# Sending part of one store over half of the DMA engines in a batched matrix product

## The chip, the cores and the metric

The kernel runs on one core of a Trainium2 chip. The metric is the device time of one execution in microseconds (us). The kernel before takes 136.39 us (median of three runs, 136.19 to 136.42). A profile times the core's own span, which is 1.7 to 1.95 us shorter than the device time of the same execution: 134.6 us for the kernel before. Whenever two spans are compared here, they are spans of single profiled executions; when two times are compared, they are medians of several executions.

## The reference

```python
def setup_inputs():
    batch, dim_i, dim_j, dim_k = 32, 256, 512, 384
    return {
        "x": np.random.randn(batch, dim_i, dim_j).astype(np.float32),
        "y": np.random.randn(batch, dim_j, dim_k).astype(np.float32),
    }

def reference(x, y):
    return np.einsum('bij,bjk->bik', x, y).astype(np.float32)
```

Thirty-two independent products, 16.8 MB of `x` and 25.2 MB of `y` read, 12.6 MB written.

## The kernel before

The 32 products are done in 16 units of two (`u` is the unit, `G = 2`). Loads and stores are all issued by SyncE in one fixed order, so they form one queue. `x` is loaded for four products at once (2 MB), `y` for one product (0.79 MB), and each unit is stored by one DMA of 128 partitions (0.79 MB). In between the inputs are rounded to 16 bits, `x` is transposed on TensorE, and the products are collected from PSUM. None of that is touched by the change.

```python
    def load(u):
        if u == 0:
            load_x(0)
        if (u + 1) * G % Q == 0 and u + 1 < U:
            load_x((u + 1) * G // Q)
        y_of[u] = y_pool.tile([P, G, NJ, K], F32, name="y_sb")
        for g in range(G):
            keep(nc.sync.dma_start(out=y_of[u][:, g],
                                   in_=y[u * G + g].rearrange("(q t) k -> q t k", q=P)))
    ...   # round_x, transpose, round_y, multiply, collect
    def store(u):
        keep(
            nc.sync.dma_start(
                out=out[u * G : (u + 1) * G].rearrange("g (m e) k -> (g m) e k", e=NE),
                in_=o_of.pop(u),
            )
        )

    ahead = LAG - 2
    for u in range(ahead):
        load(u)
    for s in range(U + 2):
        if s + ahead < U:
            load(s + ahead)
        ...   # the work of unit s - 1, and the collection of unit s - 2
        if s >= 2:
            store(s - 2)
```

Each DMA has one of eight completion semaphores, in turn: DMA n uses slot n modulo 8, and SyncE does not issue it before DMA n-8 has landed. This comes from the framework and is seen in the program; no line of the kernel says it.

## Time and profile before

| what | before |
|---|---|
| device time | 136.39 us |
| span of the profiled execution | 134.6 us |
| DMA packets, bytes | 8072, 54.64 MB |
| rate over the span | 406 GB/s |
| busiest compute engine | PE, 61% |
| last store: issued, first engine landed, last engine landed | 128.73, 131.81, 133.30 us |
| from that last landing to the end of the span | 1.33 us |

The first row is the median of the timed runs, the next four are on the page, the last from the trace's records of issues and landings. The prediction below shows the page's DMA row, the chain and the last windows. Two more lines of before turn out to matter, from the view of one source line, which here is the end of the program. The columns are the engine, the instruction and its count, then shortest/median/longest duration in ns, and the first and last start in us.

```profile
L223 SPq EVENT_SEMAPHORE  x7: 17/28/28, 129.1 to 134.6; - x7
...
L223 SPq DRAIN  x3: 7/7/130, 133.7 to 134.2; - x3
```

SyncE closes the program with waits on the completion semaphores and some drains. The first drain starts at 133.7, though the last store landed at 133.3.

### The profile page before, as it was taken

The page shows a single profiled execution, that of the slowest core. Times are in us where ns is not written, and L with a number is a line of the kernel's source. Part 1 is how long each engine was busy: PE and PEld are TensorE (multiplying, and loading weights), DVE is VectorE, ACT ScalarE, POOL GpSimd, SP SyncE. Part 2 cuts the span into 40 slices and gives each one's busy share as a digit, 9 for nine tenths or more (in the row PEclk, how much of TensorE's full clock was granted, in tenths as well). Part 3 has the DMA queues.
Part 4 walks back from the last instruction along what each step waited for, and adds up shares of the span by engine and source line. Part 5 has one row for each costly group of instructions (what it writes and reads, how often), then busy time and mean ns, then how long its engine had stood idle before and what let it go on. Part 6 is the DMA issues. An engine that isn't in the chain of part 4 may idle for free.

```text
span 134.6 us, 1741 instructions
## 1 busy us (share of the span) xinstructions
PE 82.4 (61%) x640; PEld 58.9 (44%) x640; DVE 57.6 (43%) x144; ACT 75.6 (56%) x145; POOL 0.7 (1%) x6
## 2 busy tenths in 40 slices
PE   0029496965197929785197853964469652896900
PEld 0018374854064717563164632652246531565500
DVE  0034457363633563515624256352453536427510
ACT  3046687576662876538744378552774557629600
POOL 2000000000000000000000000000000000000000
PEclk9999999999658996899757997799757998569985
DMA  5999999999999999999999999999999999999991
GB/s 112 419 403 454 403 424 421 456 392 412 420 451 410 414 427 422 455 392 418 425 444 438 400 412 427 458 403 414 425 420 443 413 414 427 420 427 422 417 405 74
DMA packets 8072, 54.64 MB, mean 406 GB/s; under 512 B 896, under 2 KB 896, under 8 KB 7040
## 3 DMA queue, kind: packets, MB, share of 16 engines
q1 hardware_dynamic: 8064, 54.53, 97.5%
q8 instruction: 5, 0.08, 0.2%
q14 instruction: 3, 0.02, 0.1%
HBM read 41.94 MB, written 12.58 MB: 405 GB/s over the span
## 4 chain that ended last, share of the span: by engine, by line
DMA 91%; PE 2%; DVE 1%; SPq 1%; issue 0%
DMA y_sb<-in_y_dram 62%; DMA x_sb<-in_x_dram 15%; DMA out_dram<-o_sb 13%; PE o_ps L145 2%; DVE o_sb L162 1%; SPq L85 0%; DVE y_r L133 0%; SPq L70 0%; SPq L167 0%
## 5 line engine op out<-in xcount | busy, mean ns | idle before, releaser
L145 PE MATMUL o_ps<-y_r,xt_sb 128*64 128x384 f16 x512 | 60.0, 400 | 29.8 <-DVE o_sb L162 27.8
L145 PEld LDWEIGHTS <-xt_sb 128*64 128x64 f16 x512 | 40.5, 133 | 45.6 <-issue 32.2
L131 ACT CAST y_r<-y_sb 128x384 f16<-128x384 f32 x64 | 29.5, 512 | 16.8 <-DMA y_sb<-in_y_dram 16.7
L133 DVE CAST y_r<-y_sb 128x384 f16<-128x384 f32 x64 | 20.0, 356 | 30.2 <-DMA y_sb<-in_y_dram 28.8
L113 PE MATMUL t_ps<-identity,x_r 128*128 128x128 f32 x128 | 23.1, 319 | 15.9 <-DVE x_r L95 15.9
L113 PEld LDWEIGHTS t_ps<-identity,x_r 128*128 128x128 f32 x128 | 18.4, 210 | 23.2 <-issue 12.8
L97 ACT CAST x_r<-x_sb 128x1024 f16<-128x1024 f32 x16 | 15.9, 1043 | 19.3 <-DMA x_sb<-in_x_dram 19.3
L123 ACT COPY xt_sb<-t_ps 128x512 f16<-128x512 f16 x32 | 17.4, 588 | 14.3 <-DVE xt_sb L121 13.9
L95 DVE CAST x_r<-x_sb 128x1024 f16<-128x1024 f32 x16 | 10.4, 690 | 25.3 <-DMA x_sb<-in_x_dram 25.3
L121 DVE COPY xt_sb<-t_ps 128x512 f16<-128x512 f16 x32 | 13.0, 422 | 13.8 <-PE t_ps L113 13.2
L162 DVE COPY o_sb<-o_ps 128x384 f32<-128x384 f32 x32 | 16.4, 549 | 1.8 <-PE o_ps L145 1.8
L160 ACT COPY o_sb<-o_ps 128x384 f32<-128x384 f32 x32 | 14.1, 500 | 1.2 <-PE o_ps L145 1.2
L97 ACT ACT_TABLE_LOAD x1 | 1.3, 1283 | 0.7 <-PEq L212 0.7
masks.py:199 POOL TENSOR_SCALAR_AFFINE_SELECT identity<-identity 128x128 f32<-128x128 f32 x1 | 0.3, 292 | 0.1
masks.py:197 POOL MEMSET identity<- 128x128 f32 x1 | 0.2, 204 | 0.3 <-POOLq L212 0.3
L212 POOL MEMSET const-bfloat16-1.0<- 128x1 bf16 x1 | 0.1, 101 | 0.0
L212 POOL MEMSET const-uint8-127<- 128x1 uint8 x1 | 0.1, 101 | 0.0
L212 POOL MEMSET const-float32-0.0<- 128x1 f32 x1 | 0.1, 98 | 0.2 <-issue 0.2
L212 POOL MEMSET const-float32-1.0<- 128x1 f32 x1 | 0.1, 98 | 0.0
## 6 DMA issues: line engine op xcount, KB each, us to landing
y_sb<-in_y_dram SPq DMA_DIRECT2D x32, 768.0 KB, 17.9
x_sb<-in_x_dram SPq DMA_DIRECT2D x8, 2048.0 KB, 20.8
out_dram<-o_sb SPq DMA_DIRECT2D x16, 768.0 KB, 17.8
```

Source lines behind the costliest of these rows:

```text
L95: keep(nc.vector.tensor_copy(xr_of[q][:, r : r + 2], x_of[q][:, r : r + 2]))
L97: keep(nc.scalar.copy(xr_of[q][:, r : r + 2], x_of[q][:, r : r + 2]))
L113: nc.tensor.transpose(t_ps[:, f, h], x_w[:, h * NE + e + f, n::NW], identity)
L121: keep(nc.vector.tensor_copy(dst[:, f], src[:, f]))
L123: keep(nc.scalar.copy(dst[:, f], src[:, f]))
L131: keep(nc.scalar.copy(yr_of[u][:, g, t], y_sb[:, g, t]))
L133: keep(nc.vector.tensor_copy(yr_of[u][:, g, t], y_sb[:, g, t]))
L145: nc.tensor.matmul(o_ps[g * M : (g + 1) * M], xt_sb[:, t // 2, e, a * PQ : (a + 1) * PQ, :, t % 2].rearrange("c p h -> c (p h)"), y_r[:, g ...
L160: keep(nc.scalar.copy(o_of[u][:, e], ps_of[u][e]))
L162: keep(nc.vector.tensor_copy(o_of[u][:, e], ps_of[u][e]))
L212: nc = _bacc.Bacc("TRN2", target_bir_lowering=False, num_devices=1)
```

## The change

The intent is to move work from the upper eight DMA engines to the lower eight. In the fifth store, the last 32 partitions go in four DMAs of 8 partitions, and a DMA of 8 partitions is to be carried by engines 0 to 7 alone (the prediction says where this comes from). The remaining 96 partitions use all sixteen.

```diff
+SHARE, SMALL = 4, 4
 ...
     def store(u):
-        keep(
-            nc.sync.dma_start(
-                out=out[u * G : (u + 1) * G].rearrange("g (m e) k -> (g m) e k", e=NE),
-                in_=o_of.pop(u),
-            )
-        )
+        o_sb = o_of.pop(u)
+        dst = out[u * G : (u + 1) * G].rearrange("g (m e) k -> (g m) e k", e=NE)
+        cuts = (0, *range(P - SMALL * 8, P + 1, 8)) if u == SHARE else (0, P)
+        for k, m in enumerate(cuts[:-1]):
+            rows = slice(m, cuts[k + 1])
+            keep(nc.sync.dma_start(out=dst[rows], in_=o_sb[rows]))
```

## The prediction

> **What bounds the kernel now.** I read the page first: the 40 slices, then the chain of work that ended last.
>
> ```profile
> PEclk9999999999658996899757997799757998569985
> DMA  5999999999999999999999999999999999999991
> GB/s 112 419 403 454 403 424 421 456 392 412 420 451 410 414 427 422 455 392 418 425 444 438 400 412 427 458 403 414 425 420 443 413 414 427 420 427 422 417 405 74
> ...
> HBM read 41.94 MB, written 12.58 MB: 405 GB/s over the span
> ## 4 chain that ended last, share of the span: by engine, by line
> DMA 91%; PE 2%; DVE 1%; SPq 1%; issue 0%
> ```
>
> The DMA row is at nine tenths in 38 of 40 slices and the rate is flat at about 423 GB/s (the windows view: 423 for 20 to 60 us, 424 for 60 to 100, 423 for 100 to 124). No compute engine is busy over 61% of the span. The reader is to see that the sixteen DMA engines are the bound from the second slice to the last but one, and that the change moves no byte more or less: 54.5 MB stay 54.5 MB. So it can matter only through which engine carries what.
>
> Then the chain in order of time:
>
> ```profile
> 34.70 17.89 DMA y_sb<-in_y_dram
> 52.58 0.02 issue
> 52.60 17.86 DMA y_sb<-in_y_dram
> 70.47 0.02 issue
> 70.48 0.03 SPq L167
> 70.51 0.03 issue
> 70.54 17.84 DMA out_dram<-o_sb
> 88.38 0.02 issue
> 88.40 20.84 DMA x_sb<-in_x_dram
> 109.24 0.02 issue
> 109.26 14.84 DMA y_sb<-in_y_dram
> 124.10 0.02 issue
> ```
>
> Each DMA is issued 0.02 to 0.07 us after an earlier one has landed. Numbering the 56 DMAs in order of issue, DMA n starts when DMA n-8 has landed on its last engine; the trace shows eight completion semaphores used in turn. About 17.9 us lie between issue and landing, so the queue is eight deep and never dry.
>
> Last, the end of the span by windows (PE, PEld, DVE, ACT, POOL busy, clock, DMA share, GB/s):
>
> ```profile
> 128.00:130.00 2.00, 0.06 (x2) 0.00 (x0) 0.56 (x1) 0.00 (x0) 0.00 (x0) 1.00 0.94 393
> 130.00:131.00 1.00, 0.00 (x0) 0.00 (x0) 0.00 (x0) 0.00 (x0) 0.00 (x0) 0.58 1.02 424
> 131.00:132.00 1.00, 0.00 (x0) 0.00 (x0) 0.00 (x0) 0.00 (x0) 0.00 (x0) 0.50 0.69 283
> 132.00:133.00 1.00, 0.00 (x0) 0.00 (x0) 0.00 (x0) 0.00 (x0) 0.00 (x0) 0.50 0.16 68
> ```
>
> The rate does not stop, it fades over about 1.5 us: the engines do not finish together. The trace keeps sixteen landing records for each DMA, one per engine, without the engine's number. For the last store but one they lie, from the earliest (129.49 us), at 0, .13, .13, .25, .30, .31, .42, .59, .72, .97, 1.37, 1.52, 1.52, 1.75, 1.76 and 1.99 us. In the first DMAs this spread is 0.65 us. It jumps to 2.06 at the eleventh DMA, after a 16,384-byte packet on the instruction queue that started at 31.74 us and took 1.09; four more such packets follow (54.6, 77.9, 103.4, 125.7 us), and more engines fall behind. As no engine is ever idle, one that has fallen behind stays behind. The last store lands first at 131.81 and last at 133.30: the slowest engine sets the end. It also sets the last y load's landing (122.16 first, 124.10 last), on which the last products, the last store's issue (128.73) and so the whole tail hang.
>
> **What the Trainium skill says.** "DMA: Bandwidth & Descriptors", section "Why a DMA increments its semaphore by 16 and not by 1", says that a DMA issued from SyncE runs on the largest number k up to 16 that divides its slowest dimension, and on the lowest-numbered k engines. So 128 and 96 partitions use all sixteen, and 8 partitions use engines 0 to 7. The trace of before agrees for 128 (sixteen landings for each DMA); it has none with 8. Section "Latency and other measured facts" of that page calls engines 7 and 15 usually slower, and holds the cause uncertain. This trace has several slow engines but no numbers for them, so it cannot confirm it; 7 and 15 lie one in each half, which would speak against a gain. "Runtime: NRT & Kernel Launch", section "Instruction fetch mechanics", says that instructions are refilled in blocks of 16 KiB by DMA; the five 16,384-byte packets agree. No page says which engine carries a refill.
>
> **The change part by part.** Removed: one store of 128 partitions, eight packets of 6,144 bytes on each of 16 engines. Such a packet takes 234 ns (median of the trace) and overlaps the next by 4, so one costs its engine 230 ns.
> - Added: a store of 96 partitions, 6 packets on each engine, and four of 8 partitions, one packet on each of engines 0 to 7. The lower half carries 10 packets instead of 8, the upper half 6. That is +2 x 0.230 = +0.46 us for each lower engine and -0.46 us for each upper one.
> - Completion writes: DMA follows DMA on an engine at 1.88 us, less 8 x 0.230 = 1.84 leaves about 0.04 each. The lower half has four more: +0.16 at most. So about +0.5 to +0.62 us below, -0.46 above.
> - Issue: four more DMA instructions on SyncE at 0.34 each, 1.4 us. SyncE stands waiting for slots most of the time here, so this costs nothing.
> - Slots: the five pieces take five of the eight. The x load now issued at 56.34 must wait for the DMA that lands at 66.79, a delay of 10.4 us. At 66.79 the queue still holds two y or store DMAs of 0.79 MB and the fifth store, 2.36 MB; at 424 GB/s that is 5.6 us. So it doesn't run dry. After the fifth store's landing at about 72.3 several slots come free together, the loads catch up, and the order is as before. No gap, no cost.
>
> What is left is the shift between the halves, early enough (the data moves at 68 to 72 us) to be carried to the end by an always full queue. Its worth depends on which half the late engines are in. If the eight latest (0.72 to 1.99) are the upper half, the upper maximum becomes 1.99 - 0.46 = 1.53 and the lower 0.59 + 0.6 = 1.2: the end comes 0.46 us earlier, at about 135.9. The lateness list splits well at that place, and a change that relieves just this half would be odd unless somebody had seen it late. I give this six or seven chances in ten. Perfect balance could not bring more than the mean lateness: 1.99 - 0.86 = 1.1 us.
>
> **The rivals.**
> - The late engines are mixed. Then the slowest of the lower half, say 1.76, becomes about 2.3 and the end comes 0.3 us later: 136.7. For it: five instruction packets would fall on one half only by some rule, none of which I can see. Against it: the intent of the edit.
> - The slowest engine is in the lower half: 1.99 + 0.6, so 137.0. Same evidence, less likely.
> - The loss of queue depth bites: a gap at 66 to 70 us. Then each us of gap is a us at the end. Against it are the 5.6 us worked out above; I give it 4%.
> - A floor beside the engines: the last store is issued at 128.73 and lands 3.08 us later even on an engine that had run dry. But its issue hangs on the last y load's slowest engine as well, so both move together. With an early y landing the gain is not eaten.
>
> **Range and chances.** Weights of 0.65 for 135.9, 0.2 for 136.7 to 137.0, and the rest near 136.4 (a partial gain, with another late engine taking over) give a mean of about 136.1. Three runs of before lie within 0.23 us, so noise adds 0.15. Eight times in ten: 135.7 to 136.9. Two per cent are 2.7 us; the shift is 0.46 and even perfect balance 1.1, so over 2% faster is all but excluded. Over 2% slower needs a dry queue.
>
> **What the changed profile would show.** Sixty DMAs on the page instead of 56; the stores' issues x20. The x load that followed the fifth store is issued at about 66.8 instead of 56.34, and the DMA row and GB/s stay flat there; a digit under 9 around 66 to 72 us would prove the rival of depth. If the upper half is the late one, the last y load lands at about 123.6 instead of 124.10, the last store is issued near 128.3, and the fade at the end is shorter by some 0.4 us. If not, the fade is longer, and the last y lands later. The prediction is wrong beyond its range if small DMAs carry a fixed cost on their engines that the 0.04 us doesn't show, or if the instruction packets fall elsewhere in the changed program.

## The result

The changed kernel takes **137.03 us** (median of six runs, 136.31 to 137.16) beside 136.34 for the kernel before (six runs, 136.19 to 136.43). The ratio is 1.0041, with a 95% interval of 1.0017 to 1.0064. A ratio is computed as the mean time of one kernel's fast runs over that of the other's of the same rounds, so it isn't quite the ratio of the medians. The kernel is slower by about half a us, where I had expected 0.3 us less.

The page of the changed kernel, the lines that answer to those in the prediction:

```profile
DMA  5999999999999999999999999999999999999991
GB/s 121 413 401 454 410 419 420 452 395 420 412 459 394 419 423 431 434 403 421 425 425 440 406 422 419 447 428 408 421 425 443 413 412 426 425 423 426 417 388 64
DMA packets 8104, 54.64 MB, mean 405 GB/s; under 512 B 928, under 2 KB 928, under 8 KB 7072
```

The DMA row is the same digit for digit, and there is no hole at 66 to 72 us (slices 20 to 22: 425, 425, 440). The 32 added packets are the completion writes of four DMAs on eight engines each; so the four small DMAs ran on eight engines, as the page of the Trainium skill on DMA that the prediction cites says. The bytes are unchanged.

The order of issue, from SyncE's timeline of the changed kernel (start, duration, line):

```profile
54.27 10.66 SPq L175 DMA_DIRECT2D out_dram<-o_sb  x5
66.54 0.37 SPq L73 DMA_DIRECT2D x_sb<-in_x_dram  x1
```

The five pieces are issued over 10.7 us, and the x load after them at 66.54 instead of 56.34, as predicted (66.8). It costs nothing, since the queue still holds work.

One warning on reading this profile. A DMA on eight engines leaves nine records on its semaphore, one about 0.45 us after the start of its issue and eight landings, instead of sixteen. The page then gives no landing for any DMA of the four semaphores that carried such a piece, 28 of the 60. Its chain of waits and its "us to landing" for the changed kernel are therefore not used here. The landing times below are the trace's own records, grouped by the number of engines of each DMA. An engine's lateness is the time from the first landing of a DMA to the landing on that engine.

The windows at the end of the changed kernel, to be set against those of before in the prediction:

```profile
130.00:131.00 1.00, 0.00 (x0) 0.00 (x0) 0.00 (x0) 0.00 (x0) 0.00 (x0) 1.00 0.99 412
131.00:132.00 1.00, 0.00 (x0) 0.00 (x0) 0.00 (x0) 0.00 (x0) 0.00 (x0) 1.00 0.82 338
132.00:133.00 1.00, 0.00 (x0) 0.00 (x0) 0.00 (x0) 0.00 (x0) 0.00 (x0) 1.00 0.19 80
```

The fade is a little later (0.82 against 0.69 of the DMA time from 131 to 132), where the prediction wanted it earlier. The last landing is at 133.37 us, 0.07 later than before. But the span is 134.88 against 134.63, 0.25 longer. So 0.18 us were lost in the tail, the time from the last landing to the end of the span. The closing lines of the changed kernel:

```profile
L227 SPq EVENT_SEMAPHORE  x7: 17/28/28, 133.4 to 134.8; - x7
...
L227 SPq DRAIN  x3: 7/7/7, 134.1 to 134.4; - x3
```

All seven semaphore waits of SyncE now start after the last landing (133.4), where before the first of them started at 129.1. The first drain is at 134.1 instead of 133.7. Here are the starts of the closing instructions, from the trace's instruction records, in us:

```
                               before    changed
last store landed              133.30    133.37
wait that the landing ended    133.32    133.39   (slot 8 of 8; slot 4 of 8)
next instruction               133.75    133.84   (a drain;     the wait on slot 5)
waits on slots 6, 7, 8         -         133.92, 133.99, 134.06
drains                         133.75, 133.94   134.13, 134.19
end of span                    134.63    134.88
```

SyncE waits for the eight slots in a fixed order. With 56 DMAs the last store has the last slot, so nothing is left to wait for. With 60 DMAs it has the fourth slot, and four more waits follow, 0.07 us each, although all are already met. (Of these 0.28 us only 0.18 show in the tail, because the first drain takes 7 ns here and 130 ns before.) In both kernels there is also a pause of about 0.43 us just after the landing; this is looked into below.

### The profile page after: what moved, and what is told of

The parts are those of the page before. It is cut to its first block, busy times and chain, and to the rows that moved or that the text cites. A ratio compares the mean times of both kernels' runs of the same rounds, so it can differ in the third digit from the quotient of the medians.

```text
span 134.9 us, 1747 instructions
## 1 busy us (share of the span) xinstructions
PE 80.8 (60%) x640; PEld 58.6 (43%) x640; DVE 57.3 (42%) x144; ACT 75.6 (56%) x145; POOL 0.7 (1%) x6
## 4 chain that ended last, share of the span: by engine, by line
DMA 82%; PE 7%; DVE 3%; SPq 2%; issue 1%
DMA y_sb<-in_y_dram 56%; DMA x_sb<-in_x_dram 15%; DMA out_dram<-o_sb 11%; PE o_ps L148 6%; SPq L88 2%; DVE o_sb L165 1%; DVE xt_sb L124 1%; SPq L73 1%; DVE y_r L136 1%; PE t_ps L116 1%; SPq L175 0%
## 5 line engine op out<-in xcount | busy, mean ns | idle before, releaser
L148 PE MATMUL o_ps<-y_r,xt_sb 128*64 128x384 f16 x512 | 57.5, 388 | 29.4 <-DVE o_sb L165 27.4
L148 PEld LDWEIGHTS <-xt_sb 128*64 128x64 f16 x512 | 39.7, 129 | 43.7 <-issue 31.6
L116 PE MATMUL t_ps<-identity,x_r 128*128 128x128 f32 x128 | 23.9, 324 | 17.9 <-DVE x_r L98 17.8
L116 PEld LDWEIGHTS t_ps<-identity,x_r 128*128 128x128 f32 x128 | 18.9, 209 | 25.4 <-issue 12.8
```

Source lines behind the costliest of these rows:

```text
L116: nc.tensor.transpose(t_ps[:, f, h], x_w[:, h * NE + e + f, n::NW], identity)
L148: nc.tensor.matmul(o_ps[g * M : (g + 1) * M], xt_sb[:, t // 2, e, a * PQ : (a + 1) * PQ, :, t % 2].rearrange("c p h -> c (p h)"), y_r[:, g ...
```

## The experiments

Theories. **A**: moving packets shifts the lateness of the two halves, and late engines are in the lower half too. **B**: the cost is in the number of DMAs (slots, completions, a shallower queue). **C**: the lateness comes from instruction refills that fall on fixed engines. **D**: part of the cost is in the closing instructions.

### Is it the shift or the number of pieces?

The first batch, with eleven runs of the kernel before (median 136.47).

**e1_even**: the same number of pieces, each over all sixteen engines.

```diff
-        cuts = (0, *range(P - SMALL * 8, P + 1, 8)) if u == SHARE else (0, P)
+        cuts = (0, *range(P - SMALL * 16, P + 1, 16)) if u == SHARE else (0, P)
```

> The fifth store in five DMAs again (64 partitions, then four of 16), so as many DMAs and completion slots as in the changed kernel, but each piece runs on all sixteen engines: 4 + 4 x 1 = 8 packets on each, no shift between the halves. Theory A (the cost of the change is the two extra packets on each lower engine, which lengthens the work of an engine that is already late): no different from before, 136.3 to 136.5 us. Theory B (the cost is the four added DMAs: completions, slots, a shallower queue): as slow as the changed kernel, 136.9 to 137.1.

Measured: 137.34 us, ratio 1.0048 (1.0023 to 1.0072). Theory A, as I had put it, missed: pieces without a shift are as slow as the change. The trace gives three parts. The pieces themselves cost almost nothing: from the y load before the store to the x load after it, the mean landing of the engines moves by 6.79 us, against 6.71 before; the latest engine's moves by 6.73 against 6.72. The closing instructions cost 0.21 us. The rest, 0.76 us of the profiled execution, came at 126 us, long after the store, when an instruction refill fell on an engine that was already 1.36 us late and made it 2.82. So this kernel is slow for reasons other than its pieces.

**e2_two**: the change made in the fifth and in the tenth store.

```diff
-        ... if u == SHARE else (0, P)
+        ... if u in (SHARE, SHARE + 5) else (0, P)
```

> The same cut of a quarter into four DMAs of 8 partitions, in the fifth and in the tenth store: twice the shift, four packets more on each lower engine, four fewer on each upper one. Theory A: the late lower engine is 1.1 us later than in the kernel before, the end comes 1.1 to 1.3 us later, about 137.5; the landing records of the last stores are spread over more than 3 us. Theory B: also about 137.7, but without that spread. The late engines being all in the upper half (my prediction): below 136.

Measured: 137.20 us, ratio 1.0051 (1.0019 to 1.0084). The expected 137.5 was roughly met, but not with theory A's sign: the last store but one is spread over 2.15 us, not over more than 3. The second cut is close to the end, and the loads behind it were issued later: the first y load after that store, which the kernel before issues at 98.86 us, is issued at 109.79. Its windows from 112 to 118 us (last columns: clock, DMA share, GB/s):

```profile
112.00:114.00 2.00, 0.59 (x3) 0.28 (x3) 0.92 (x4) 1.17 (x4) 0.00 (x0) 0.55 1.08 399
114.00:116.00 2.00, 0.62 (x5) 0.42 (x7) 1.70 (x5) 1.93 (x5) 0.00 (x0) 0.50 0.96 396
116.00:118.00 2.00, 2.00 (x16) 1.31 (x14) 0.26 (x1) 0.61 (x2) 0.00 (x0) 0.50 1.02 399
```

The kernel before has in the same windows:

```profile
112.00:114.00 2.00, 0.00 (x0) 0.00 (x0) 1.01 (x4) 1.07 (x4) 0.00 (x0) 0.77 1.02 427
114.00:116.00 2.00, 1.11 (x8) 0.81 (x10) 1.21 (x3) 1.82 (x4) 0.00 (x0) 0.50 1.02 427
116.00:118.00 2.00, 2.00 (x16) 1.30 (x14) 0.63 (x2) 0.93 (x2) 0.00 (x0) 0.50 1.01 421
```

27 GB/s are missing over 6 us, 0.16 MB or 0.4 us of the full rate. I first took this for the rival of queue depth, but a dry queue is not what the trace shows: the DMA share of these windows is 1.02 on average in both kernels, and the page of e2 has no digit under 9 there:

```profile
DMA  5999999999999999999999999999999999999992
```

What differs is the length of packets. Between 112 and 122 us, 18 packets of 6,144 bytes took 0.4 to 2.3 us instead of 0.234, in all 8.2 us more, or 0.5 us for each of the sixteen engines; the kernel before has none there. Why they took longer, and whether the late issue has a part in it, is not shown. At this cut too the shift is seen: between the y loads around it the latest landing moved by 4.17 us instead of 3.72, the earliest by 3.22 instead of 3.68. The last store lands at 134.31, 1.0 us later than before; but its span is only 0.5 longer, as its tail is 0.83 us instead of 1.33. That was the first sign of theory D: with 64 DMAs the last store has the last slot again, and the pause is gone.

**e3_half**: two small DMAs instead of four (`SHARE, SMALL = 4, 2`).

> Two DMAs of 8 partitions instead of four, in the fifth store only: half the shift, one packet (0.23 us) more on each lower engine. Theory A with a slowest engine in the lower half: 0.25 to 0.35 us over before, about 136.65. If the slowest is in the upper half and the next, 0.2 to 0.3 us earlier, in the lower: within 0.1 us of before.

Measured: 136.53 us, ratio 1.0012 (0.9988 to 1.0036), no difference from before. The time fits the second branch of what was expected, but the trace does not: at the cut the latest engine, 1.71 us late, was in the lower half and the next, 1.61, in the upper. The latest landing was pushed out by 0.24 us there, half of what four pieces do (see the table below), and still the last store landed at 133.30, as before. So the shift at the cut did not reach the end in this trace.

**e4_map**: the kernel before with tiny loads that name the engines.

```diff
+        for k in ((2 * u - 5, 2 * u - 4) if 3 <= u <= 9 else (15,) if u == 10 else ()):
+            mark = const_pool.tile([k, 128], F32, name=f"mark{k}")
+            keep(nc.sync.dma_start(out=mark, in_=x[0][:k, :128]))
```

> The kernel before with fifteen tiny loads of 1, 2, ... 15 partitions of 512 bytes between the fourth and the eleventh store. A DMA of m partitions should run on engines 0 to m-1, so that its landing records name the engines by number, one more with each load. If a DMA has k landings for k partitions, the numbering holds. Theory A: among the six latest engines, some have numbers under 8. My prediction: all of them are 8 to 15. Time about 136.4 to 137, which says nothing here.

Measured: 136.31 us, one execution. Each load of m partitions had exactly m engine landings (beside the record at its issue), for m from 1 to 15. A tiny load queues behind the store ahead of it, so its landings show the lateness of engines 0 to m-1; the one that is new with each m is engine m-1. At about 87 us engine 1 was 1.3 us late, engine 3 1.2, engine 5 1.6 and engine 6 2.0; the latest of all, at 2.2, was not among engines 0 to 7 and was named as engine 14 by the last of the loads. Engine 12 joined them with 1.8 us after the refill at 103.5 (a refill is a packet of 16,384 bytes on the instruction queue). So four of the six latest engines are in the **lower** half. My prediction had all of them in the upper.

### Is it fixed which engines are late?

The second batch, with eleven more runs of the kernel before (median 136.52).

**e5_map_again**: e4's kernel once more.

> The same kernel as the first map once more. The sixteen engines' lateness by number is read again. Theory C (each 16 KiB instruction refill is given to one engine, the same in every execution of one program): refills fall on engines 14, 5, 6, 12 and 10 again, as in the first map. If the engine is drawn anew in each execution: other numbers.

Measured: 136.54 us, one execution. Engine 14 was 1.9 us late, engine 6 2.05, engine 12 1.74 after the refill at 104 us, and engines 1, 3 and 5 1.4, 0.9 and 1.4. The big ones are the same engines as in the first map (the last refill, at 125.8 us, comes after the last tiny load, so that no load names its engine). So in two executions of one program the refills fell on the same engines. That speaks for theory C within one program. It can't be told whether another program has the same engines; the next experiments suggest that it hasn't.

**e6_even_again**: e1's kernel once more.

> The fifth store in 64 + 4 x 16 partitions again. Theory C: 136.7 to 137.5 as before, and the trace again shows the last refill on an engine that was already 1.3 to 1.4 us late. Drawn anew: the median falls to about 136.6 (before plus 0.16 for four completions on each engine), or the trace shows other engines hit.

Measured: 136.97 us, ratio 1.0032 (1.0014 to 1.005). Both batches agree that this kernel is slow; of twelve executions in all, ten took 136.74 us or more. But in this trace the latest engine was 0.4 us later than in the kernel before already at the y load ahead of the cut store (70.88 us against 70.47), so what made it late lies outside the edited store. And the last refill fell on an engine that was 0.8 to 0.95 us late, not 1.3 to 1.4: the sign that theory C asked of the trace is missing, though the time fits it.

**e7_after_again**: the changed kernel once more.

> The changed kernel again. Theory A with the engine drawn anew: again a spread of 136.3 to 137.2, low where the latest engine is in the upper half and high where it is in the lower. Theory C: the trace shows the same engines late as in the first trace: 1.05, 1.54 and 1.70 in the lower half, 1.76 in the upper.

Measured: 137.04 us, ratio 1.0036 (1.002 to 1.0051). The result stands. Theory C's sign is missing: the two latest engines, 1.68 and 1.59 us, are now both in the upper half, and the latest of the lower half is 1.12 us late. (The first piece landed on the latest lower engine only 0.12 us after the engine of 1.59 had landed the 96 partitions; a packet takes 0.234, so that engine carried no piece.) If the latest two engines are those hit by the two refills before the cut, the refills did not fall on the same engines in two executions of one program.

**e8_before_again**: the kernel before, as a control.

> The kernel before, as a control: a ratio to itself within 0.2% of 1. Its trace shows whether the refills fall on five different engines again (spread at the end near 2.0 us) and whether its slow executions, one of seventeen so far over 137, are those in which a refill falls on an engine that is already late.

Measured: ratio 1.0009 (0.9992 to 1.0026). Its trace repeats the first one closely: the latest engine of the last store but one lands at 131.48 in both, the last store at 133.29, the tail is 1.34. Its slowest execution, 136.99, has no trace, so the question about slow executions stays unanswered.

With two traces of each kernel, the shift can be read at the place where it happens. The table has, for the y load before the fifth store and the x load after it, how much later the latest engine and the earliest one landed, in us. The fourth column tells where the two latest engines were, from the landings of the 8-partition pieces.

| kernel | latest engine | earliest engine | the two latest engines |
|---|---|---|---|
| before, two traces | +6.72, +6.76 | +6.69, +6.70 | not known |
| even, two traces | +6.73, +6.70 | +6.72, +6.73 | not known |
| changed, two traces | +7.20, +7.45 | +6.30, +6.31 | one upper, one lower; both upper |
| half (e3) | +6.96 | +6.56 | the latest lower, the next upper |
| changed twice (e2), first cut | +6.27 | +6.42 | both upper |
| changed, with drains (e10 below) | +6.48 | +6.31 | both upper |

The arithmetic of the prediction holds here: an upper engine gains 0.46 us (6.70 to 6.31, nearly), a lower one loses about 0.5. In the changed kernel the latest engine before the cut was in the upper half, 1.76 us late in the first trace and 1.68 in the second. In the first trace a lower one, 1.70 us late, was close behind it. So the upper engine was relieved, the lower one took its place, and the latest landing was pushed out by 0.48 us. In the second trace the latest lower engine was only 1.12 us late, and the shift alone would have left the latest landing about where it was. It was pushed out by 0.69 us because two packets on that lower engine took 0.72 and 0.89 us instead of 0.234 and 0.611, 0.77 us in all (in the second trace the mean of all engines moved out by 0.2 us as well: between 69 and 71 us seven packets of 6,144 bytes took 0.54 to 0.98 us instead of 0.234). In the other two traces where both latest engines were upper, the latest landing came 0.45 and 0.24 us earlier, as I had hoped for all. The even pieces move neither. Of such long packets of 6,144 bytes, over 0.4 us between 68 and 74 us, there were none in five traces without a cut (two of before, the two maps, e9), one in three traces of the even cut, and one to seven in each of the five fast traces with pieces of 8 partitions. So the uneven pieces may have a cost at the cut beside the shift; no run separates the two.

Not all of that reaches the end. The traces differ by more than that before the cut: at the y load ahead of it the latest engine landed at 70.47 and 70.45 us before, at 70.19 and 70.30 in the changed kernel, and at 70.26 to 70.88 in the other traces of fast executions. The latest engine of the last store but one landed at 131.48 before, at 131.55 and 131.91 in the two traces of the changed kernel, and the last store at 133.30, 133.37 and 133.70.

### What the closing instructions cost

The third batch, with eleven runs of the kernel before (median 136.48). The pause of 0.43 us sits at a fixed place counted from the start of SyncE's program, after the 79th of its instructions in the trace. In before that is between the last wait and the drain. The changed and the even kernel have four DMAs more, and there it lies four instructions further from the end, between the waits on slots 4 and 5; e3_half has two more, and there it lies two further. In the maps, with fifteen more, it falls among the last loads and stores (115.44 to 115.86 us in the first), long before the end. An 8,192-byte instruction packet follows it: at 134.38 us before, 134.68 in the changed kernel, 119.1 in the first map. To test this I put 16 drains into SyncE's program, near its start, where it waits for slots: no data, no DMA, no slot.

```diff
     for u in range(ahead):
         load(u)
+    for _ in range(16):
+        keep(nc.sync.drain())
```

**e9_before_drain**: the kernel before with the drains.

> The kernel before with 16 drain instructions on SyncE after its first loads, where SyncE would stand waiting anyway. They move no data, add no DMA and no slot; they only make SyncE's program 16 instructions longer, so that the place where it pauses 0.43 us (in both traces of before: between the last landing's wait at 133.31 and the drain at 133.75) falls among the earlier DMA issues. Theory D (part of the change's cost is in the closing instructions): last landing unchanged near 133.30, span about 0.45 to 0.5 us shorter, 136.0 us. If the pause belongs to the landing and not to the place in the program: 136.5 as before.

Measured: **136.15 us**, ratio 0.9965 (0.9952 to 0.9978), faster than both kernels. The last store lands at 133.51, no earlier than before (133.30), and still the span is 134.3: the tail is 0.83 us instead of 1.33. The closing lines:

```profile
L225 SPq EVENT_SEMAPHORE  x7: 17/28/28, 129.3 to 134.3; - x7
...
L225 SPq DRAIN  x3: 7/7/7, 133.6 to 133.9; - x3
```

The first drain follows the landing by 0.08 us, not by 0.45. The 8,192-byte packet is now at 108.6 us. So the pause belongs to a place in the program, as theory D says. That it is the crossing into the next block of instructions is my reading of the packet that moves with it.

**e10_after_drain**: the changed kernel with the drains.

> The changed kernel with the same 16 drains. Theory D: 0.43 us faster than the changed kernel, about 136.6. Four closing waits still follow the last landing, as its last store uses the fourth of the eight slots: 0.27 us more than in the kernel before with drains. What is left over that, if anything, is lateness of the engines (theory A: 0.1 to 0.4 us).

Measured: 136.78 us, ratio 1.0016 (1.0004 to 1.0028). The tail falls from 1.51 to 1.09 us, so by the 0.43 expected; the median by 0.26, across batches.

```profile
L229 SPq EVENT_SEMAPHORE  x7: 17/28/28, 133.6 to 134.6; - x7
...
L229 SPq DRAIN  x3: 7/7/7, 133.9 to 134.2; - x3
```

Again all seven waits lie behind the landing (133.53), and with the pause gone they show alone: the drain comes at 133.88, 0.33 us after the wait that the landing ended, against 0.07 in e9. So the four extra waits cost 0.26 us. The tail is 0.83 us in e9 and in e2_two, whose last store has the last slot, and 1.09 in e10 and e11 (below), where it has the fourth.

**e11_even_drain**: the even cut with the drains.

> The even cut, 64 + 4 x 16 partitions, with the same 16 drains: as many DMAs, slots and closing waits as the changed kernel, but no shift between halves. Theory A (the shift costs): 0.1 us over the kernel before with drains plus 0.27 for the closing waits, about 136.4, and 0.2 to 0.4 below the changed kernel with drains. Theory D alone: equal to the changed kernel with drains.

Measured: 136.49 us, ratio 1.0008 (0.9986 to 1.003); five of six executions between 136.25 and 136.64, one at 137.42. In its trace the last store lands at 133.39, 0.09 later than before, and the tail is 1.09. The times are what theory A asked of it: 0.34 above e9, of which 0.26 are the closing waits, and 0.29 below the changed kernel with drains. The two intervals overlap, so the 0.29 is a hint, not a proof; the last landings, 133.39 and 133.53, differ by half of it.

**e12_after_merge_drain**: the changed kernel with drains and four joined y loads, to get back to 56 DMAs and the last slot.

```diff
+        if u in range(8, 12):
+            keep(nc.sync.dma_start(
+                out=y_of[u],
+                in_=y[u * G : (u + 1) * G].rearrange("g (q t) k -> q g t k", q=P)))
+            return
```

> The changed kernel with drains, and with the two y loads of four later units (ninth to twelfth) each joined into one DMA: 56 DMAs again, so the last store is back on the last of the eight slots and no closing wait follows it. The bytes and packets on each engine are those of the changed kernel. Theory D: the 0.27 us of the closing waits go, and the kernel equals the kernel before with drains, about 136.0. Theory A: it stays 0.1 to 0.4 us above that, with the last landing that much later.

Measured: 136.81 us with all runs, ratio of the fast runs 1.0018 (0.9998 to 1.0038). The one profiled execution, 138.94 us, was slow: around the cut store, from 69.1 to 73.7 us, 15 packets of 6,144 bytes took 0.45 to 1.8 us instead of 0.234, and the latest engine came to be 5.5 us late. No other trace shows this to such a degree; a milder form is in e7 and in the second cut of e2. The five fast executions lie between 136.39 and 137.28. On theory A the experiment doesn't decide anything: its times are too scattered, and it has no trace of a fast execution. For the closing waits even the slow trace serves, as they come after the last landing: the tail is 0.83 us, as in e9.

## Why the prediction was right or wrong

Of the theories, A holds where the store is cut, with the lower engine's loss in the measured size, but the way from there to the end is argued and not shown; of B what D makes of it is left, and a dry queue was seen in no run; C fits the two maps, but the signs that it asked of the second traces of the even cut and of the changed kernel are missing; D is shown, the pause by moving it and the closing waits by the tails of 0.83 and 1.09 us.

**"Within 2%"** was right, and for the stated reason: the bytes don't change, and the shift of 0.46 us is small beside 2.7. The point of 136.1 was too low by 0.9 us, and the measured median, 137.03, lies 0.1 above the range's upper end of 136.9. The direction was wrong. (The prediction's own weights give 136.17, not 136.1.)

**The arithmetic of the shift was right.** "+0.46 us for each lower engine and -0.46 us for each upper one", and 0.5 to 0.62 with the completions. Measured: 0.40 us gained by the earliest (upper) engine, 0.48 lost at the latest one in the first trace, when a lower engine had come to be it (the 0.69 of the second trace contains long packets).

**The step that failed is the premise on who is late**: "If the eight latest (0.72 to 1.99) are the upper half", to which I gave six or seven chances in ten. The trace of before has no engine numbers; I took the place from a gap in the sorted list and from the edit's intent; the list does not even split there, with 0.13 us between the eighth and the ninth engine and 0.40 between the tenth and the eleventh. The maps show engines 1, 3, 5 and 6 among the six latest, and only 12 and 14 in the upper half, in a program with fifteen loads more; the changed kernel's own first trace has engines of 1.05, 1.54 and 1.70 us in the lower half beside one of 1.76 in the upper. The first rival came nearest: "The late engines are mixed. Then the slowest of the lower half, say 1.76, becomes about 2.3 and the end comes 0.3 us later: 136.7." In the first trace the lower engine was 1.70 us late, and the latest landing at the cut was pushed out by 0.48 us; half the shift (e3) pushed it out by 0.24. In the second trace the lower engine was 1.12 us late, still enough to eat the gain, and two long packets on it made the 0.69; this is the prediction's own sign of being wrong, a cost of small DMAs that the 0.04 us does not show, if the pieces caused them. The last landing of the program came 0.07 and 0.40 us later. That this is because of the cut is not shown: the even cut, without a shift, was as slow, and e3's 0.24 us did not reach the end.

**A term was missing from the sum**: the closing instructions. The prediction said of the slots "No gap, no cost". There was no gap, but four more DMAs move the last store from the last slot to the fourth, and the tail grew from 1.33 and 1.34 to 1.51 in both traces, 0.18 us. This adds up: 0.07 + 0.18 = 0.25 us in the first pair of spans (134.88 against 134.63), and 0.41 + 0.17 = 0.58 in the second (135.21 against 134.63). The median differs by 0.69 and 0.52 in the two batches, near the second pair.

**Queue depth**: the 5.6 us of work in hand were enough. For one cut the rates show no dip. For the second cut of e2_two they do, but with the engines as busy as before and longer packets, so a dry queue is not shown there either.

**Still open**: why the even cut without drains took 137.06 us in the median of its twelve executions. Its closing instructions explain 0.2 us and its pieces less than 0.1. In both its traces the rest comes from refills or lateness outside the edited store. With the drains the excess was gone. I suspected that each program has its own assignment of refills to engines and that this one's is unlucky. The two maps fit this, but the second traces of the even and of the changed kernel speak against it, so it stays open. The same holds for the changed kernel: how much of the 0.3 to 0.5 us that it loses beside the 0.18 of the tail comes from the shift, how much from long packets, and how much from lateness elsewhere, no run separates.

## What to carry to other kernels

Before shifting work between parallel engines, find out which of them are late: a few tiny DMAs of 1, 2, 3, ... partitions name them by number, for the cost of one run. Where the DMA queue is full to the end, look at the instructions after the last landing as well: adding DMAs, even free ones, can change which completion is waited for last and where a pause in the issuing engine's program falls; here 16 drains in a place where the engine waits anyway were worth 0.35%, about what I had hoped for from the change (0.46 us). And a cut into small DMAs is paid for in completion slots: with several us of work queued the rate showed no dip after one cut, while a second one nearer to the end came with 0.16 MB less in 6 us.

## What the Trainium skill lacked or had wrong

- "DMA: Bandwidth & Descriptors", section "Latency and other measured facts", names engines 7 and 15 as usually slower and ties its guess at the cause to descriptor rings that DMAs issued from SyncE do not have, which the prediction left out. So it bears on this kernel little, and nothing here contradicts it: in the first map engine 7 was about 0.5 us late and engine 15, by elimination, about 0.75. The section lacks the lateness that was found here, 2.2 us for engine 14 and 2.0 for engine 6.
- "Runtime: NRT & Kernel Launch", section "Instruction fetch mechanics", calls the cost of crossing a block of instructions mostly hidden. In this kernel each 16,384-byte refill made one DMA engine about 1.5 us later than it was (from about 0.5 to 2.06 us at the first), and as the queue is never dry it stayed late to the end. A pause of 0.43 us in SyncE after its 79th instruction, such a crossing by my reading, stood openly in the tail. The page also has no 8,192-byte packets, of which this trace has three, and doesn't say which DMA engine carries a refill.
- "DMA: Bandwidth & Descriptors", section "Rules for kernel authors", says that transfers under 64 KB are mostly overhead. In a full queue four pieces of 48 KB moved the engines' mean landing by 6.76 and 6.92 us in the two traces of the changed kernel instead of 6.71, so 0.05 and 0.2 us in all.
- No page has the price of a semaphore wait that is already met at the end of a program: 0.07 us each on SyncE.
